# Where the projection of group C's gate stands: in group B's stage or in group A's

## The chip, the cores and the metric

One core of a Trainium2 chip runs the kernel. It has five engines with instruction queues of their own: TensorE (PE: matmuls, with its weight loads shown as PEld), VectorE (DVE), ScalarE (ACT), GpSimd (POOL) and SyncE (SP), which here issues the DMAs. Each engine works through its queue in the order in which the program wrote it. The metric is device time in microseconds (us); the median of three runs before the change is 951.26 us (949.56 to 951.63).

## The reference

Two layers of one mixer block over 512 latent tokens and 256 context tokens of width 1024. Each layer normalizes and modulates its input, projects it once to 3584 columns, and runs three kinds of attention on slices of the result: A (differential, 4 heads), B (grouped-query, 6 heads, 2 key-value heads), C (neighbourhood attention with a bias, 6 heads). Each group's output is multiplied by a gate of its own:

```python
qa, ka, va, ga, qb, kb, vb, gb, qn, kn, vn, gn = split_proj(h @ w_in[l])
...
yn = neighbourhood_attend(qn, kn, vn.reshape(b, s, C_HEADS, HEAD_DIM), kn_c, vn_c, nat_rpb[l], rows)
yn = yn * jax.nn.silu(gn)
y = jnp.concatenate([ya, yb, yn], axis=-1) @ w_out[l]
x = x + gt[:, None] * y
```

`gn` is the gate of group C: 384 columns of the projection. It needs nothing but the normalized input, and nobody needs it before C's attention is multiplied by it. In the first layer the context tokens go through everything too; in the second they only give keys and values.

## The kernel before

Tokens are cut into tiles of 128: tiles 0 to 3 are latent, 4 and 5 context. The projection is cut into chunks of columns: `a0`, `a1` (A's keys, queries, values), `ga`; `b0` (B's keys and values), `b1` (B's queries), `gb`; `c0` (C's keys), `c1` (C's values), `c2` (C's queries), `gn`. A chunk over one tile is 24 matmuls of 128x384 (8 blocks of the inner dimension, three products of split operands each: lines 684, 685, 686), a "tile" of projection below. In layer 0 `gn` has 6 tiles, in layer 1 it has 4.

After a tile's matmuls its evacuation follows. Of queries and keys: ACT copies (L467) and squares (L469), DVE sums (L470), and after every second tile one reciprocal root on POOL (L155), a scaling on DVE (L503), the split into two fp16 halves on ACT (L520, L528) and DVE (L521), and a DMA transpose issued by SP (L539). Of a gate: a tanh on ACT (L605), one DVE operation (L607) and a store to `g_d` in DRAM (L611); the attention loads it back tile by tile (L973 to L977).

A layer runs in stages. Stage A runs A's attention with the chunks of list `FA` as filler, stage B runs B's attention with `FB`, stage C runs C's attention with the output projection (`op`). The function `both` pulls filler in proportion to the attention's units: one call of `next(f)` is two inner blocks (six matmuls) of a tile. C's stage needs `c0`, `c1`, `c2` complete. In layer 0 C's attention begins with the context tiles, in layer 1 with latent rows that lie in query tiles 0 and 1.

An attention unit is: scores on TensorE (L780, `sc`) into one of two PSUM buffers, a maximum on DVE (L832, L835), the exponential on ACT (L849, which frees the scores' buffer), a split of the result into two halves (ACT L869, POOL L870 or DVE), a DMA transpose (L872, `pt<-hl`), and products with the values (L905, L906, `pv`).

Weights come through one stream: the chunks' order in `ORDER` (from the lists) is the order of 384 KB loads (L68), of the rounding on ACT (L81) and of the rest on POOL (L84), with six split pieces alive at most. Adaptive modulation (`ada`, L235 and L242; loads at L220) is a third kind of filler: while stage B of layer 0 runs, one block of it follows every second tile of projection (`st["cad"]` is 2 there and 0 in stage A), and what is left is done between stage B and stage C.

The order of the instructions on each engine is set ahead of time by a scheduler that runs its own model of the program with priorities (scores of attention come first, at -400). So a line moved in a list moves many rows.

Of the kernel before, what the change touches and what calls it, by code (L numbers as in the profile page):

```python
# [108 lines left out]
def tile_hybrid_block(ctx: ExitStack, tc: tile.TileContext, xT_d, cT_d, ng_d, w_ada, bT_d, w_in, w_out,  # L109
# [152 lines left out]
    }  # L262
    FA = ["b0", "b1", "gb"]
    FB = ["c0", "c1", "c2", "gn"]
    FC = ["y", "o"]
    YE = 2
    F1 = ["a1", "ga"]
    ORDER = [c for c in ["a0"] + F1 + FA + FB + FC if c in CH]
    VCOL = {"a0": (256, 384), "a1": (0, 128), "b0": (128, 256), "c1": (0, 384)}
# [789 lines left out]
    def both(l, g, chunks, lead=0):  # L1059
        share.phase = g  # L1060
        f = fill(l, chunks)
        nf = n_quanta(l, chunks)
        na = len(units(l, g)) + 4
        for _ in range(lead):
            next(f, None)
        done = [lead]

        def pump():
            next(f)
            done[0] += 1  # L1070

        st["pump"] = pump
        for x, _ in enumerate(attn(l, g)):
            want = min(nf, lead + (nf - lead - REST.get(g, 0)) * (x + 1) // (na - (YE if g == "B" else 0)))
            while done[0] < want:
                next(f, None)
                done[0] += 1
            if g == "B" and done[0] >= nf and st.get("y") != l:
                run(f)
                open_y(l)  # L1080
                st["y"] = l
        run(f)
# [115 lines left out]
    if True:  # L1198
# [50 lines left out]
        for l in range(DEPTH):  # L1249
# [3 lines left out]
            st["cad"] = AK[l][2]  # L1253
            both(l, "A", FA)
            st["cad"] = AK[l][3]
            both(l, "B", FB)
            while st["done"] < (24 if l == 0 else 32):
# [103 lines left out]
```

## Time and profile before

| | us |
|---|---|
| median of 3 runs | 951.26 |
| profiled execution | 952.01 |
| its span | 950.2 |
| PE busy | 834.0 |
| POOL busy | 642.8 |
| DVE busy | 652.6 |
| ACT busy | 589.5 |

The span is the time from the first to the last instruction of the profiled execution; its own time is 1.8 us longer. Busy times of an engine are sums over its instructions, with overlaps counted once. In the span layer 0 has stage A from about 108 to 264 us, stage B to about 375 and C's scores from 406; layer 1 has stage A from 624 to 739, B to 825 and C's scores from 845. The gates of C were evacuated at 388 to 425 us in layer 0 and at 840 to 866 in layer 1. In timeline rows the columns are start, length, engine, line, operation, output and inputs, and in brackets the idle time just before and who ended it. In rows of waits they are the waiting line, the one waited for, and us in total, times and longest.

### The profile page before, as it was taken

Reading aid. Unit: us, or ns where it says so; the run is one execution under the profiler, and the core shown is the slowest. Engines: PE = TensorE matmul, PEld = TensorE weight load, DVE = VectorE, ACT = ScalarE, POOL = GpSimd, SP = SyncE. Lnnn points to the kernel's source line nnn. Section 1 sums busy time; section 2 is a strip of 40 time slices with the busy share of each in tenths; the row PEclk is TensorE's granted clock in tenths of the full one; section 3 lists DMA queues with packets and bytes.
Section 4 is the critical chain, followed back from the end, with each engine's and each line's share of the span. In section 5 each row is a group of like instructions: output and inputs, shape, how many; then the busy total and the mean of one; then the engine's idle time right before and its main releaser. Section 6 shows DMA issues by size and latency. Waiting matters only on the chain.

```text
span 950.2 us, 17943 instructions
## 1 busy us (share of the span) xinstructions
PE 834.0 (88%) x6386; PEld 713.8 (75%) x6386; DVE 652.6 (69%) x1246; ACT 589.5 (62%) x1269; POOL 642.8 (68%) x562
## 2 busy tenths in 40 slices
PE   6799888979798979797999879988869999987998
PEld 4689668868676869785778669967758777875777
DVE  4977687878587577357655776567987876676543
ACT  5334587767686758476653434468868787867630
POOL 1759957997788566445444347978998995855640
PEclk8999999999899989897999978989988999998999
DMA  9925897656868977999899613467647788989732
GB/s 311 314 85 134 211 200 158 132 107 149 177 130 196 199 182 175 241 234 214 191 233 237 208 60 79 112 171 151 133 118 170 154 181 175 263 216 243 140 91 89
DMA packets 361449, 165.47 MB, mean 174 GB/s; under 512 B 256656, under 2 KB 355216, under 8 KB 361104
## 3 DMA queue, kind: packets, MB, share of 16 engines
q1 hardware_dynamic: 361360, 164.33, 73.5%
q8 instruction: 50, 0.82, 0.4%
q14 instruction: 39, 0.32, 0.1%
HBM read 86.55 MB, written 15.47 MB: 107 GB/s over the span
## 4 chain that ended last, share of the span: by engine, by line
PE 26%; POOL 10%; DMA 9%; DVE 7%; issue 4%; ACT 4%; SPq 1%; DVEq 0%; POOLq 0%; ACTq 0%
DMA pt<-hl 6%; POOL hl L870 3%; PE proj L684 3%; PE sc L780 3%; PE proj L686 3%; PE proj L685 3%; POOL wlo L84 2%; PE op L1092 2%; PE op L1094 2%; PE op L1093 2%; PE pv L905 2%; DVE mx L835 1%; ACT p L849 1%; DVE xn L503 1%; POOL rsqb L155 1%
## 5 line engine op out<-in xcount | busy, mean ns | idle before, releaser
L870 POOL TENSOR_TENSOR hl<-p,hl 128x768 f16<-128x768 f32 (+3 forms) x138 | 205.1, 1490 | 135.8 <-ACT hl L869 115.2
L84 POOL TENSOR_TENSOR wlo<-raw,whi 128x768 fp32r<-128x768 f32 (+1 forms) x104 | 184.9, 1786 | 52.6 <-ACT whi L81 31.2
L684 PE MATMUL proj<-whi,bigL 128*128 128x384 f32 (+1 forms) x592 | 203.7, 345 | 9.7 <-DVE tb L607 3.7
L685 PE MATMUL proj<-wlo,bigL 128*128 128x384 f32 (+1 forms) x592 | 199.6, 337 | 1.8 <-POOL wlo L84 1.7
L686 PE MATMUL proj<-whi,bigL 128*128 128x384 f32 (+1 forms) x592 | 196.2, 334 | 0.0
L849 ACT ACTIVATE p<-sc,nb,gsc 128x768 f32<-128x768 f32 (+3 forms) x200 | 166.9, 845 | 26.1 <-DVE p L865 14.9
L835 DVE TENSOR_REDUCE mx<-sc 128x1 f32<-128x768 f32 (+2 forms) x128 | 118.5, 930 | 32.1 <-PE sc L780 30.8
L684 PEld LDWEIGHTS proj<-whi,bigL 128*128 128x128 f32 x592 | 115.5, 195 | 19.7 <-DVE tb L607 5.7
L869 ACT CAST hl<-p 128x768 f16<-128x768 f32 (+3 forms) x144 | 104.0, 724 | 40.8 <-DMA pt<-hl 38.0
L685 PEld LDWEIGHTS proj<-wlo,bigL 128*128 128x128 f32 x592 | 115.9, 196 | 5.0 <-POOL wlo L84 2.9
L686 PEld LDWEIGHTS proj<-whi,bigL 128*128 128x128 f32 x592 | 114.8, 195 | 2.3 <-issue 1.0
L905 PEld LDWEIGHTS <-pt 128*128 128x128 f16 x736 | 68.0, 102 | 52.1 <-DMA pt<-hl 37.9
L81 ACT CAST whi<-raw 128x768 fp32r<-128x768 f32 (+1 forms) x104 | 80.7, 779 | 39.7 <-DMA raw<-in_w_in_dram 21.3
L684 PE MATMUL proj<-whi,bigC 128*128 128x384 f32 (+2 forms) x224 | 75.3, 336 | 7.0 <-ACT bigC L433 5.8
L685 PE MATMUL proj<-wlo,bigC 128*128 128x384 f32 (+2 forms) x224 | 73.6, 329 | 0.0
L905 PE MATMUL pv<-vA,pt 128*128 128x128 f16 (+2 forms) x424 | 53.8, 232 | 22.4 <-DMA pt<-hl 22.3
L155 POOL TENSOR_TENSOR rsqb<-rsqb,half 128x12 f32<-128x12 f32 (+2 forms) x25 | 70.4, 2815 | 3.2 <-DVE rsqb L154 2.9
L686 PE MATMUL proj<-whi,bigC 128*128 128x384 f32 (+2 forms) x224 | 72.5, 328 | 0.0
L906 PEld LDWEIGHTS <-pt 128*128 128x128 f16 x736 | 68.3, 102 | 3.3 <-issue 0.9
L780 PE MATMUL sc<-bigL 128*128 128x512 f16 (+4 forms) x184 | 47.6, 321 | 23.4 <-ACT p L849 20.5
L837 ACT ACTIVATE nb<-mx,lnp,gsc 128x1 f32<-128x1 f32 (+1 forms) x104 | 39.9, 385 | 35.1 <-DVE mx L835 30.5
L503 DVE TENSOR_TENSOR xn<-xn,rsqb 128x384 f32<-128x384 f32 (+1 forms) x44 | 48.6, 1130 | 15.0 <-POOL rsqb L155 10.8
(319 smaller groups left out, 2028.1 us busy)
## 6 DMA issues: line engine op xcount, KB each, us to landing
raw<-in_w_in_dram SPq DMA_DIRECT2D x56, 384.0 KB, 4.0
adw<-in_w_ada_dram SPq DMA_DIRECT2D x68, 256.0 KB, 3.7
raw<-in_w_in_dram SPq DMA_DIRECT2D x24, 256.0 KB, 3.1
raw<-in_w_out_dram SPq DMA_DIRECT2D x16, 384.0 KB, 4.7
g_d<-tb SPq DMA_DIRECT2D x20, 192.0 KB, 2.6
gt<-g_d SPq DMA_DIRECT2D x18, 192.0 KB, 2.9
hl<-in_w_ada_dram SPq DMA_DIRECT2D x12, 256.0 KB, 5.0
pt<-in_w_ada_dram SPq DMA_DIRECT2D x12, 256.0 KB, 5.0
```

What stands on the lines that cost most here:

```text
L81: self.nc.scalar.copy(out=hi, in_=raw2)
L84: self.share("W").tensor_tensor(out=lo, in0=raw2, in1=hi.bitcast(F32), op=ALU.subtract)
L155: G.tensor_tensor(out=y, in0=x, in1=half[:, 0:n], op=ALU.pow)
L684: PE.matmul(ps, lhsT=xh, rhs=hi, start=(kt == 0), stop=False)
L685: PE.matmul(ps, lhsT=xh, rhs=lo, start=False, stop=False)
L686: PE.matmul(ps, lhsT=xl, rhs=hi, start=False, stop=(kt == KT - 1))
L780: PE.matmul(ps, lhsT=q, rhs=k, start=n == 0, stop=n == b[2] - 1)
L835: V.tensor_reduce(out=mx[:, 0:ns], in_=ps[:, 0:w * ns].rearrange("p (a b) -> p a b", b=w), axis=AX.X, op=ALU.max)
L849: A.activation(out=p[:, w * x:w * x + w], in_=u["ps", i][:, w * x:w * x + w], func=AF.Exp, bias=u["nb", i][:, x:x + 1], scale=lc[l]["sc"][ ...
L869: A.copy(out=hl[:, 0:n], in_=p)
L870: lo_eng.tensor_tensor(out=hl[:, n:2 * n], in0=p, in1=hl[:, 0:n], op=ALU.subtract)
L905: PE.matmul(po[r, :], lhsT=pt[:, b, r], rhs=V_[:, vt, c0:129], start=first, stop=False)
```

## The change

The chunk `gn` goes from the end of `FB` to the end of `FA`. Nothing else changes in the text.

```diff
-    FA = ["b0", "b1", "gb"]
-    FB = ["c0", "c1", "c2", "gn"]
+    FA = ["b0", "b1", "gb", "gn"]
+    FB = ["c0", "c1", "c2"]
```

It changes what follows from the lists: stage A of layer 0 has 96 pieces of filler for its attention where it had 72, stage B has 72 where it had 96 (72 and 56, 64 and 80 in layer 1). The weights of `gn` are loaded and split ahead of those of `c0`. Stage B of layer 0 has 18 tiles of projection instead of 24, so nine modulation blocks instead of twelve come in it, and three more between B and C.

ACT, layer 0, where A's attention ends and B's begins. `sq<-proj` is the tanh of a gate tile, `xn<-proj` the copy of a tile of keys or queries, `nb<-mx,lm` belongs to A's attention and `nb<-mx,lnp` to B's. Before:

```order
L467 COPY xn<-proj 128x384
L864 ACTIVATE dn<-dn 128x1
L869 CAST hl<-p_3077 128x256
L469 ACTIVATE sq<-xn 128x384
L837 ACTIVATE nb<-mx,lm,gsc 128x2
L849 ACTIVATE p_3159,dn<-sc,nb,gsc 128x256 x2
L528 CAST stg<-xn 128x768
L862 ACTIVATE dn<-dn,lm 128x1
...
L837 ACTIVATE nb<-mx,lnp,gsc 128x1
```

After:

```order
L849 ACTIVATE p_3280,dn<-sc,nb,gsc 128x256 x2
L862 ACTIVATE dn<-dn,lm 128x1
L837 ACTIVATE nb<-mx,lm,gsc 128x2
L864 ACTIVATE dn<-dn 128x1
L849 ACTIVATE p_3327,dn<-sc,nb,gsc 128x256 x2
...
L605 ACTIVATE sq<-proj 128x384
L869 CAST hl<-p_3327 128x256
L837 ACTIVATE nb<-mx,lnp,gsc 128x1
```

The copies of `c0` that stood among the last units of A (L467, L469, L528) have given their place to the tanh of `gn` (L605); `c0` comes behind the first units of B.

PE, layer 0, ahead of the first score of C (`sc<-bigC`). Before, the last of 33 matmuls of `gn` in a row:

```order
L684 MATMUL proj<-whi,bigL 128x384
L685 MATMUL proj<-wlo,bigL 128x384
L686 MATMUL proj<-whi,bigL 128x384
L780 LDWEIGHTS bigC
L780 MATMUL sc<-bigC 128x256
```

After, behind the last matmul of `c2`, one modulation block and 20 attention products:

```order
L242 MATMUL ada<-sel,adt 128x2
L235 MATMUL ada<-adw,cS 32x128 x4
L623 MATMUL yt<-ident,o 128x128 x3
L235 MATMUL ada<-adw,cS 32x128 x4
L242 MATMUL ada<-sel,adt 128x2
L235 MATMUL ada<-adw,cS 32x128 x8
L242 MATMUL ada<-sel,adt 128x2
L235 MATMUL ada<-adw,cS 32x128
L645 MATMUL yt<-ident,xn 128x128 x4
L235 MATMUL ada<-adw,cS 32x128 x3
L780 LDWEIGHTS bigC
L780 MATMUL sc<-bigC 128x256
```

Between `c2` and C's first score stood 81 matmuls of `gn`; now modulation blocks and a few transposes of finished output rows (`yt`) stand there.

SP, layer 0, at the transposes of the last two tiles of `c2` (`bigC<-stg`). After the change:

```order
L220 DMA adw<-in_w_ada_dram 128x4x128
L68 DMA raw<-in_w_out_dram 128x3x256
L643 DMA xn<-o_d_79 128x256 x2
L220 DMA adw<-in_w_ada_dram 128x4x128
L539 DMA_TRANSPOSE bigC<-stg 128x6x128
L220 DMA adw<-in_w_ada_dram 128x4x128
L539 DMA_TRANSPOSE bigC<-stg 128x6x128
```

Before, a load of finished rows stood ahead of each of the two (L643); now a load of a modulation block does (L220), which waits until TensorE is done with the block before it.

## The prediction

> **What bounds the kernel now.** The page's shares come first.
>
> ```profile
> PE 834.0 (88%) x6386; PEld 713.8 (75%) x6386; DVE 652.6 (69%) x1246; ACT 589.5 (62%) x1269; POOL 642.8 (68%) x562
> ```
>
> TensorE is busy 88% of 950.2 us. A share over the whole span says little, so the second view is busy time by stage: layer 0 stage A (108 to 264), stage B (to 375), the passage to C (to 406.4), stage C; then layer 1 stage A, stage B, the passage, stage C and tail.
>
> ```profile
> 108.00:264.00 156.00, 133.20 (x1037) 117.99 (x1036) 120.82 (x204) 114.67 (x295) 129.17 (x126) 0.96 0.72 157
> 264.00:375.00 111.00, 99.33 (x802) 83.41 (x801) 79.50 (x144) 79.89 (x138) 77.23 (x57) 0.95 0.83 179
> 375.00:406.40 31.40, 26.43 (x220) 24.78 (x220) 14.23 (x26) 14.94 (x28) 14.44 (x9) 0.89 1.06 239
> 406.40:520.00 113.60, 103.71 (x851) 82.64 (x851) 70.26 (x164) 68.37 (x146) 55.67 (x51) 0.95 0.94 219
> 624.00:739.00 115.00, 92.46 (x663) 81.51 (x664) 93.55 (x143) 89.05 (x210) 101.17 (x99) 0.91 0.66 146
> 739.00:825.00 86.00, 80.60 (x612) 68.77 (x611) 59.70 (x81) 68.28 (x112) 70.86 (x50) 0.98 0.83 185
> 825.00:845.00 20.00, 17.52 (x142) 15.93 (x139) 15.32 (x19) 13.66 (x24) 16.42 (x9) 1.00 0.80 224
> 845.00:950.00 105.00, 94.23 (x699) 76.36 (x696) 55.49 (x127) 51.60 (x109) 41.20 (x32) 0.93 0.67 152
> ```
>
> First number after the stretch: its length, then PE busy, PEld, DVE, ACT, POOL. TensorE idles 22.8 us in stage A of layer 0 and 22.5 us in that of layer 1, where POOL (129 and 101 us) and DVE are nearly as busy, but only 11.7 and 5.4 us in stage B. So B is TensorE's, and A is shared. The third view, who TensorE waited for, tells what A's idle time is; the first two rows are layer 0's A, the next two layer 1's.
>
> ```profile
> PE pv L905 <- DMA pt<-hl: 9.3, 7, 4.3
> PE sc L780 <- ACT p L849: 4.4, 3, 2.4
> ...
> PE sc L780 <- ACT p L849: 11.8, 7, 4.2
> PE pv L905 <- DMA pt<-hl: 7.3, 4, 3.0
> ```
>
> These are waits of attention's own instructions, which stand at the head of TensorE's queue; projections behind them can't pass. More projection in the stage fills such a wait only if the written order puts it ahead of the waiting score.
>
> **The change part by part.** It removes nothing and adds nothing: 144 matmuls in layer 0 (6 tiles of 24) and 96 in layer 1, their gate evacuations (ACT tanh, DVE multiply, one store each) and four weight pieces per layer stand elsewhere. TensorE has the same work; its end moves only with its idle time. So the sum below is a ledger of idle time.
>
> *Stage A.* The order shows that gn does not go into A's holes. Before, when gb was through, TensorE went on with c0 while A's attention ran out: 83 projection matmuls stand between gb and B's first score in layer 0, 57 in layer 1. Now gn stands there: 99 and 58. The scores of A hold their places between the same tiles (A's last unit in layer 0 after 72 of these matmuls before, after 76 now). So the 22.8 and 22.5 us stay, 0 is gained, and everything from c0 on comes one gate later. Bounds: a gain of 4 where the few more matmuls meet a wait, a loss of 2 from twice as many gate tiles in a row.
>
> *What a gate weighs.* In layer 0, gn's first two tiles ran from here to the next attention product:
>
> ```profile
> 380.13 0.34 PE L686 MATMUL proj<-whi,bigC 128*128 128x384 f32 x1
> 382.74 0.42 PE L684 MATMUL proj<-whi,bigC 128*128 128x384 f32 x1
> 391.82 0.42 PE L235 MATMUL ada<-adw,cS 128*32 128x128 f32 x8 [0.36 <-DMA adw<-in_w_ada_dram]
> 406.34 1.25 PE L780 MATMUL sc<-bigC 128*128 128x256 f16 x9
> ```
>
> 380.13 is the last matmul of c2, 382.74 the first of gn; 48 of them and three products end at 391.5 (391.82 less 0.36), about 4.2 us a tile: 25 us in layer 0. The fourth row is C's first score. In these 25.9 us TensorE did 81 of gn's 144 matmuls, and attention's last products. They cover the way of c2's last tiles to C's scores, which begin with the context queries, c2's tiles 4 and 5:
>
> ```profile
> 381.64 0.48 ACT L467 COPY xn<-proj 128x384 f32<-128x384 f32 x1
> 383.81 2.91 ACT L992 ACTIVATE stB<-stB,gsc 128x768 f32<-128x768 f32 x3 [1.69 <-DMA stB<-in_btab_dram]
> 386.63 0.51 ACT L469 ACTIVATE sq<-xn 128x384 f32<-128x384 f32 x1
> 387.17 0.55 DVE L470 TENSOR_REDUCE ss<-sq 128x6 f32<-128x384 f32 x1 [4.13 <-ACT sq L469]
> 389.80 2.27 POOL L155 TENSOR_TENSOR rsqb<-rsqb,half 128x12 f32<-128x12 f32 x1
> 392.10 1.03 DVE L503 TENSOR_TENSOR xn<-xn,rsqb 128x384 f32<-128x384 f32 x2 [3.08 <-POOL rsqb L155]
> 394.51 0.50 ACT L520 CAST stg<-xn 128x384 f16<-128x384 f32 x1
> 396.16 0.54 DVE L521 TENSOR_TENSOR stg<-xn,stg 128x384 f16<-128x384 f32 x1
> 398.92 1.21 SPq L539 DMA_TRANSPOSE bigC<-stg  x1
> bigC<-stg SPq DMA_TRANSPOSE x12, 3.3
> ```
>
> From 380.4 to the landing at 398.92 + 1.21 + 3.3 = 403.4 it takes 23 us. Its own instructions, without waits, are 0.5 + 0.5 + 0.55 + 0.2 + 2.3 + 1.0 + 0.5 + 1.3 + 0.5 + 1.2 + 3.3 = 12 us. These are the bounds of the chain. In the new order the scaling of the bias table stands earlier (it cost 4.5 us here), but both transposes stand on SP's queue behind loads that wait, one after the other, for the modulation blocks on TensorE, and the second cast stands behind an evacuation of yt. I take 17 us, near the middle.
>
> *Layer 0, B to C.* c2 is now last in B. Behind it TensorE has 20 products (0.9 us by 31 in 1.4 us at 380.97), four modulation blocks (about 1.0 each, by the two rows below) and 7 transposes (about 1.3, by 0.60 for 4 at 859.50): 6.2 us.
>
> ```profile
> 380.97 0.23 PE L905 MATMUL pv<-vB,pt 128*128 128x129 f16 x1
> 380.40 0.64 PE L235 MATMUL ada<-adw,cS 128*32 128x128 f32 x16
> 382.35 0.33 PE L242 MATMUL ada<-sel,adt 128*128 128x2 f32 x2
> 859.50 0.60 PE L645 MATMUL yt<-ident,xn 128*128 128x128 f32 x4
> ```
>
> The hole is 17 - 6.2 = 10.8 us (5.8 to 16.8). The other 63 matmuls of gn (11 us) filled C's first waits; what stands there now are transposes of rows that come by DMA: 2 us more idle (0 to 6). The 5.0 us that TensorE now idles from 375 to 406.4 go. Three modulation blocks that were spread over B come together, but lie inside the hole. Together +7.8 us (+0.8 to +17.8). C's first score would come at 380.4 + 25.2 + 4.0 (88 products moved ahead) + 17 = 427, 20 us later than before, and C gets most of that back, as the 63 matmuls, 48 products and two blocks that it had to do are done.
>
> *Layer 1.* C begins with latent rows, which need c2's tiles 0 and 1 only, and tiles 2 and 3 stand between.
>
> ```profile
> 823.80 0.46 ACT L467 COPY xn<-proj 128x384 f32<-128x384 f32 x1
> 841.78 1.29 SPq L539 DMA_TRANSPOSE bigL<-stg  x1
> 844.74 0.38 PE L780 MATMUL sc<-bigL 128*128 128x256 f16 x2 [2.40 <-DVE xn L503]
> 866.67 1.11 PE L645 MATMUL yt<-ident,xn 128*128 128x128 f32 x4 [3.44 <-DVE tb L607]
> ```
>
> The chain took 21 us here. The new cover is 48 matmuls, 60 products and a turn, 8.5 + 2.6 + 0.6 = 11.7 us. With 17 the hole is 5.3 (0 to 9.3). The wait of 2.4 for the same transpose is in it and goes, and so does the 3.4 us wait of yt for gn's evacuation. A hole also costs clock:
>
> ```profile
> 703.40:706.80 3.40, 0.00 (x0) 0.00 (x0) 3.20 (x3) 1.25 (x3) 3.40 (x2) 0.84 0.28 43
> 713.60:717.00 3.40, 2.46 (x17) 2.19 (x18) 2.42 (x3) 2.86 (x8) 3.40 (x4) 0.50 0.91 70
> 720.40:724.00 3.60, 3.60 (x31) 3.18 (x31) 3.44 (x6) 1.12 (x3) 2.19 (x3) 1.00 0.64 164
> 395.00:398.00 3.00, 0.59 (x2) 0.50 (x2) 1.83 (x5) 0.01 (x1) 0.16 (x1) 0.52 1.12 288
> ```
>
> After an idle stretch the granted clock was 0.50 and came back to 1.00 once TensorE had been busy. Work of 1.7 us loses as much again; I take 1 us for layer 1. In layer 0 the passage has such a stretch already (0.52 at 395). The Trainium skill, "TensorE: Matmul & The Clock Gate", Part 1, says that the clock is halved after an idle window of about 3.4 us and released after a busy one, which speaks against any change that opens a hole; the rows agree. By that rule both holes would pay 1.7 us, an estimate of 1.7 + 0.7 = 2.4 us over my sum. Layer 1: 5.3 - 2.4 - 3.4 + 1 = +0.5 us (-5.8 to +5.2).
>
> *Stage B's own waits* shrink a little, since products stand further behind their scores: -1 us (-3 to 0).
>
> Sum: 0 + 7.8 + 0.5 - 1 = **+7.3 us**. The profiled execution took 952.01 us for its span of 950.2, 0.75 over the median of 951.26, so the difference is added to the median: **958.5 us**. All low ends together give -12, all high ends +25.
>
> **Rivals.** *The chain is covered (faster).* ACT and DVE have little else at the end of B now, so the chain could run at 12 us, and C's early waits need not grow. Then layer 0 is 5.8 + 0 - 5.0 = +0.8, layer 1 0 - 5.8, B -3: -8, 943 us. For it: DVE was busy 14.2 of 31.4 us there. Against: SP's queue and a DMA share of 1.06.
>
> *A takes gn into its idle time*, as the words of the change say. If half of the 45.3 us in both layers were filled, the time would be 929 us. Against it is the order of the scores. A part of it sits in the faster case's chance.
>
> *TensorE isn't the bound (no change).* If C's pace is attention's, and the passage's hole is work that waited elsewhere anyway, the changes cancel within 0.2% (1.9 us, about what a measurement of this kernel can tell): 951 us. The Trainium skill, "Perfetto Trace Analysis", Identifying the Most-Contended Engine, says that matmul busy share misleads and weight-load share is the measure. That share is 75% here, 83.4 of 111 us in stage B. By it TensorE would have room, and this case a better chance. Against: in layer 1's passage there is no gap but the one of 2.4 us.
>
> *C doesn't get its time back (much slower).* C starts 20 us later in layer 0 and some 15 in layer 1 (12.4 of work moved ahead, less 2.4, plus 5.3); if its units go at attention's own pace, half of the 16 us of moved work in layer 0 and a third of the 12 in layer 1 are not recovered: 7.3 + 8 + 4 = +19, 970 us. It decides once C's scores wait for ACT rather than TensorE; from 420 to 520 that wait is this one row, which speaks against it.
>
> ```profile
> PE sc L780 <- ACT p L849: 2.2, 1, 2.2
> ```
>
> **How the numbers follow.** Forecast (+2 to +15) 0.52; much slower 0.12; no change 0.15; faster 0.21. So slower 0.64, same 0.15, faster 0.21, and the likeliest is 958.5, in its own range 953.5 to 966. To leave out 2 in 10 the range runs from 945 (the covered chain less some) to 971 (the much slower case).
>
> **What would show it.** In the changed profile: a TensorE gap of 6 to 17 us ahead of C's first score in layer 0, with c2's last transposes landing just before; that score at about 427; gate evacuations at about 245 to 285 and not at 388 to 425; idle time of A unchanged within 4 us in both layers; a gap under 9 us ahead of layer 1's first C score; C from first score to end shorter by 10 to 16 us. I am wrong if A's idle time falls by 10 us or more, if the gap in layer 0 is under 5 us, or if C takes as long as before.

## The result and the profile after

The changed kernel took 959.48 us (median of 12 runs) where the kernel before took 951.44 us beside it: a ratio of 1.0074, 95% interval 1.0045 to 1.0103. One of the twelve runs, 973.87 us at a mean granted clock of 0.81 where the others read 0.93 to 0.95, was in a slower state of the chip and is left out of the ratio, which is one of means. By the ratio the change is slower by 7.0 us, by the medians by 8.0; 958.5 us was forecast. The amount is right. Its place is not, as the following shows.

The profiled execution of the change took 957.69 us, its span 955.9. The shares on its page hardly differ:

```profile
PE 836.5 (88%) x6386; PEld 714.3 (75%) x6386; DVE 638.0 (67%) x1246; ACT 588.9 (62%) x1269; POOL 634.5 (66%) x562
```

The view of busy time by stage tells more. The stretches are cut at first and last scores: layer 0's stage A, B, the passage from B's last score to C's first, C to the end of the layer; then layer 1 to C's first score, and C. Columns as before (length, PE, PEld, DVE, ACT, POOL, clock, DMA share, GB/s). The change:

```profile
108.70:264.10 155.40, 133.42 (x1032) 116.95 (x1032) 123.08 (x204) 111.68 (x289) 120.14 (x122) 0.99 0.67 156
264.10:373.20 109.10, 103.23 (x863) 88.95 (x863) 70.63 (x139) 81.22 (x138) 82.06 (x61) 1.00 0.90 188
373.20:423.20 50.00, 33.69 (x305) 28.27 (x304) 22.66 (x52) 21.20 (x42) 18.91 (x11) 0.83 0.98 233
423.20:624.10 200.90, 181.75 (x1322) 153.13 (x1320) 128.21 (x285) 104.46 (x234) 112.12 (x101) 0.92 0.66 165
624.10:857.90 233.80, 203.92 (x1514) 180.35 (x1515) 164.08 (x250) 175.28 (x354) 190.80 (x159) 0.93 0.73 173
857.90:955.90 98.00, 86.30 (x593) 67.16 (x593) 54.61 (x117) 47.80 (x99) 35.55 (x28) 0.85 0.53 127
```

The same cuts of the kernel before, from C of layer 0 on (the first three differ by under 1 us from rows shown with the prediction):

```profile
406.30:624.20 217.90, 198.09 (x1465) 167.80 (x1463) 138.42 (x306) 111.23 (x246) 119.45 (x105) 0.93 0.71 175
624.20:844.70 220.50, 190.32 (x1407) 165.94 (x1407) 168.21 (x241) 170.99 (x344) 188.25 (x156) 0.95 0.74 168
844.70:950.20 105.50, 94.49 (x699) 76.62 (x699) 55.79 (x128) 51.60 (x109) 41.20 (x32) 0.93 0.67 151
```

Layer 1 begins at 624.1 us with the change and at 624.2 before. So in these two executions layer 0 lost nothing, though its C began 17 us later, and all of the difference in span, 5.7 us, came up in layer 1: 331.8 us against 326.0.

The hole ahead of layer 0's first C score is there, and larger than forecast. TensorE's timeline in the changed kernel, with c2's last matmul and the score at the ends:

```profile
400.58 0.34 PE L686 MATMUL proj<-whi,bigC 128*128 128x384 f32 x1
410.81 0.65 PE L235 MATMUL ada<-adw,cS 128*32 128x128 f32 x8 [8.15 <-DMA adw<-in_w_ada_dram]
414.69 0.66 PE L235 MATMUL ada<-adw,cS 128*32 128x128 f32 x8 [0.45 <-DMA adw<-in_w_ada_dram]
416.36 0.66 PE L235 MATMUL ada<-adw,cS 128*32 128x128 f32 x8 [1.02 <-DMA adw<-in_w_ada_dram]
421.02 0.61 PE L235 MATMUL ada<-adw,cS 128*32 128x128 f32 x2 [3.00 <-DMA adw<-in_w_ada_dram]
423.18 0.61 PE L780 MATMUL sc<-bigC 128*128 128x256 f16 x2
```

12.6 us of idle time in brackets, all for loads of the left-over modulation blocks, of 16.3 us that TensorE idles in the whole passage. SP's own timeline in the same stretch shows c2's two transposes standing among these loads:

```profile
405.65 0.93 SPq L220 DMA_DIRECT2D adw<-in_w_ada_dram  x2
...
417.18 0.38 SPq L220 DMA_DIRECT2D adw<-in_w_ada_dram  x1
417.61 1.76 SPq L539 DMA_TRANSPOSE bigC<-stg  x1
419.46 0.53 SPq L220 DMA_DIRECT2D adw<-in_w_ada_dram  x1
420.03 1.25 SPq L539 DMA_TRANSPOSE bigC<-stg  x1
```

The second transpose is issued at 421.3 and lands some 2 us later, so the last block and the last transpose are done together.

The first left-over block also held c2's own chain. The root for c2's last two tiles ended on GpSimd at 407.5 us, but their scaling (L503) began on VectorE at 413.5. Ahead of it in VectorE's queue stood the evacuation (L628) of three transposes (L623), and on TensorE these stand behind the block that waited 8.15 us for its load:

```profile
405.22 2.27 POOL L155 TENSOR_TENSOR rsqb<-rsqb,half 128x12 f32<-128x12 f32 x1 [0.35 <-DVE rsqb L154]
411.40 0.90 PE L623 MATMUL yt<-ident,o 128*128 128x128 f32 x3
412.33 0.48 ACT L627 CAST bigC<-yt 128x384 fp32r<-128x384 f32 x1 [8.36 <-PE yt L623]
412.85 0.56 DVE L628 TENSOR_TENSOR bigC<-yt,bigC 128x384 fp32r<-128x384 f32 x1 [6.92 <-ACT bigC L627]
413.52 2.04 DVE L503 TENSOR_TENSOR xn<-xn,rsqb 128x384 f32<-128x384 f32 x2
```

In layer 1 the waits ahead of C's first scores are smaller:

```profile
853.89 0.88 PE L623 MATMUL yt<-ident,o 128*128 128x128 f32 x3 [2.51 <-DVE o L950]
857.89 0.58 PE L780 MATMUL sc<-bigL 128*128 128x256 f16 x2 [3.12 <-DMA bigL<-stg]
```

### The profile page after: what moved, and what is told of

It is laid out like the page before. It is cut to its first block, busy times and chain, and to the rows that moved or that the text cites. A ratio compares the mean times of both kernels' runs of the same rounds, so it can differ in the third digit from the quotient of the medians.

```text
span 955.9 us, 17984 instructions
## 1 busy us (share of the span) xinstructions
PE 836.5 (88%) x6386; PEld 714.3 (75%) x6386; DVE 638.0 (67%) x1246; ACT 588.9 (62%) x1269; POOL 634.5 (66%) x562
## 4 chain that ended last, share of the span: by engine, by line
PE 25%; DVE 9%; DMA 8%; POOL 6%; issue 6%; ACT 5%; SPq 1%; DVEq 0%; POOLq 0%; ACTq 0%
PE proj L684 3%; PE sc L780 3%; PE proj L685 3%; PE proj L686 3%; POOL hl L870 2%; PE op L1092 2%; ACT p L849 2%; PE op L1093 2%; PE op L1094 2%; DMA pt<-hl 2%; DMA raw<-in_w_in_dram 2%; DMA adw<-in_w_ada_dram 2%; DVE xn L503 1%; POOL wlo L84 1%; PE pv L905 1%
## 5 line engine op out<-in xcount | busy, mean ns | idle before, releaser
L870 POOL TENSOR_TENSOR hl<-p,hl 128x768 f16<-128x768 f32 (+3 forms) x138 | 202.3, 1470 | 130.8 <-ACT hl L869 122.6
L686 PEld LDWEIGHTS proj<-whi,bigL 128*128 128x128 f32 x592 | 114.5, 194 | 2.4 <-issue 1.1
L905 PEld LDWEIGHTS <-pt 128*128 128x128 f16 x736 | 65.9, 99 | 36.6 <-DMA pt<-hl 18.9
L906 PEld LDWEIGHTS <-pt 128*128 128x128 f16 x736 | 66.6, 100 | 4.2 <-issue 1.4
L780 PEld LDWEIGHTS <-bigL 128*128 128x128 f16 (+2 forms) x344 | 24.7, 103 | 42.5 <-issue 30.7
```

The lines of the kernel that those rows point to most:

```text
L686: PE.matmul(ps, lhsT=xl, rhs=hi, start=False, stop=(kt == KT - 1))
L780: PE.matmul(ps, lhsT=q, rhs=k, start=n == 0, stop=n == b[2] - 1)
L870: lo_eng.tensor_tensor(out=hl[:, n:2 * n], in0=p, in1=hl[:, 0:n], op=ALU.subtract)
L905: PE.matmul(po[r, :], lhsT=pt[:, b, r], rhs=V_[:, vt, c0:129], start=first, stop=False)
```

## The experiments

Times are medians; ratios are of means, to the kernel before that ran beside them, with 95% intervals. So a ratio isn't the quotient of two medians of the table.

| kernel | time, us | ratio | layer 0, us | layer 1, us |
|---|---|---|---|---|
| before | 951.44 | 1 | 516.0 | 326.0 |
| the change | 959.48 | 1.0074 (1.0045 to 1.0103) | 515.4 | 331.8 |
| gn in A in layer 0 alone | 951.23 | 0.9978 (0.9958 to 0.9998) | 521.9 | 323.0 |
| gn in A in layer 1 alone | 956.77 | 1.0041 (1.0022 to 1.0060) | 515.7 | 329.7 |
| change, three blocks in A | 950.81 | 0.9972 (0.9949 to 0.9996) | 511.9 | 329.4 |
| change, c2 early, three blocks in A | 943.30 | 0.9891 (0.9858 to 0.9924) | 497.2 | 330.4 |
| layer 1 alone, c2 early there | 959.40 | 1.0068 (1.0039 to 1.0097) | 516.5 | 330.0 |
| before, three blocks left over | 954.26 | 1.0016 (0.9993 to 1.0039) | 512.1 | 328.7 |
| before, c2 early | 937.70 | 0.9830 (0.9797 to 0.9863) | 504.7 | 325.4 |
| change, c2 early | 953.76 | 1.0003 (0.9977 to 1.0029) | 506.7 | 329.9 |
| the change again | 953.33 (one) | | 515.2 | 328.4 |
| before, c2 early, gn in C in layer 1 | 936.65 | 0.9838 (0.9815 to 0.9861) | 501.3 | 326.3 |
| before, c2 early, three blocks in A | 934.97 | 0.9816 (0.9791 to 0.9841) | 501.9 | 325.0 |
| gn in A in layer 0 alone, c2 early, three blocks in A | 936.68 | 0.9851 (0.9813 to 0.9890) | 499.2 | 326.9 |

"Layer 0" is, in each profiled execution, from layer 0's first score of A to layer 1's, and "layer 1" from there to the end. One execution each: three of the same layer 0 (before, and the two edits of layer 1 alone) read 515.7 to 516.5, three of the changed one 515.2, 515.4 and 521.9. The execution profiled need not be typical: that of "change, c2 early" took 946.52 us, the shortest of its twelve. Since the scheduler plans everything anew, an edit in one layer also reorders rows of the other. The layer 0 of the edit in layer 1 alone has TensorE's rows in the order of before, and that of the edit in layer 0 alone has them in the order of the change. Their layers 1 have the lists of the change and of before, but many rows stand in another order there.

**Layer 0 alone, layer 1 alone.** The lists were made per layer (the diff shows the lists alone, and the comment gives the second kernel; the order of the weights and the calls of the stages follow them):

```diff
-    FA = ["b0", "b1", "gb"]
-    FB = ["c0", "c1", "c2", "gn"]
+    IN_A = {0: 1, 1: 0}      # and {0: 0, 1: 1}
+    FAL = {l: ["b0", "b1", "gb"] + ["gn"] * IN_A[l] for l in range(DEPTH)}
+    FBL = {l: ["c0", "c1", "c2"] + ["gn"] * (1 - IN_A[l]) for l in range(DEPTH)}
```

> gn moves to stage A in layer 0 alone; layer 1 as before the change. The prediction's sum put +7.8 us into layer 0's passage from B to C and +0.5 into layer 1. Theory (the lost cover in layer 0's passage): the loss of about 8 us stays whole, 957 to 961 us, with the same TensorE waits for modulation loads of 10 us or more ahead of C's first score. Rival (the loss comes from layer 1, where the changed profile shows waits of 2.5 and 3.1 us ahead of C's first scores): 951 to 954 us.

> gn moves to stage A in layer 1 alone. Theory (layer 0 holds the loss): within 3 us of before, 949 to 954 us. Rival (layer 1): 955 us or more.

The theory fell in both. With gn moved in layer 0 alone the time was 0.22% under before, with the hole in place: C's first score at 423.7 us, as in the change. With gn moved in layer 1 alone it was 0.41% over. Stage B and the passage of the kernel changed in layer 0 alone:

```profile
265.10:374.70 109.60, 103.53 (x864) 89.03 (x863) 72.55 (x139) 81.11 (x139) 81.71 (x61) 1.00 0.90 188
374.70:423.70 49.00, 33.82 (x305) 28.26 (x303) 22.70 (x52) 21.32 (x42) 19.28 (x11) 0.83 0.99 234
```

Stage B has 6.1 us of idle TensorE time where it had 11.7, and the clock is 1.00 where it was 0.95. The profile of the change reads 5.9 and 1.00.

The two edits don't add up to the change: -0.22% and +0.41% make +0.19%, about 2 us, where the change has 7. In the profile of the edit in layer 0 alone layer 0 is even 5.9 us longer than before, and it is layer 1, with the lists of before in another order, that is 3.0 us shorter. So these two runs don't show that the move costs nothing in layer 0; they show that the time of a kernel with the hole need not be over that of before.

**The left-over modulation blocks.** Three blocks of layer 0 are done in stage A, one after every eighth tile, on top of the change; and, the other way round, the kernel before leaves three over to be done behind stage B:

```diff
-AK = [[6, 2, 0, 2], [0, 1, 0, 2]]
+AK = [[6, 2, 8, 2], [0, 1, 0, 2]]
```

```diff
-                if st["cad"] and st["n"] % st["cad"] == 0:
+                if st["cad"] and st["n"] % st["cad"] == 0 and not (l == 0 and share.phase == "B" and st["done"] >= 21):
```

> The change, with three modulation blocks of layer 0 done in stage A (one after every eighth tile), so that none is left over between B and C. In the changed profile TensorE waited 12.6 us for modulation loads ahead of C's first score. Theory 1 (c2 is last and its chain to the transposes is bare, the loads only fill the same time): a hole stays, 8 us or more of idle time or of waits for c2's transposes, C's first score 15 us or more behind c2's last matmul, 955 to 960 us. Theory 2 (the three blocks left over make the hole, as each load waits for the block before, and c2's transposes stand behind these loads on SP's queue): TensorE idles under 5 us there, C's first score comes within 14 us, 949 to 954 us.

> Before the change, but with three modulation blocks of layer 0 left over for the passage from B to C, as the change leaves them; gn stays at the end of stage B. Theory 1 (the blocks' loads cost where nothing covers them): here gn covers them, 949 to 955 us. Theory 2 (the left-over blocks cost by themselves, by late modulation or by SP's queue): 956 us or more.

With the blocks in stage A the change is 0.28% under before, and 1.0% under itself. Its waits from 366 us to C's first score, and that score:

```profile
PE yt L623 <- DMA xn<-o_d: 4.4, 4, 2.0
PE yt L645 <- DMA xn<-o_d: 4.2, 3, 1.9
PE pv L905 <- DMA pt<-hl: 1.3, 2, 0.8
```

```profile
399.80 0.34 PE L686 MATMUL proj<-whi,bigC 128*128 128x384 f32 x1
418.34 0.84 PE L780 MATMUL sc<-bigC 128*128 128x256 f16 x3
```

Both theories were half right. The score still comes 18.2 us behind c2's last matmul, as theory 1 had it: c2's chain is bare. But TensorE works meanwhile, since the transposes of finished rows (`yt`) moved up to where the blocks had stood; it waits 8.6 us for their loads, in small pieces, and idles 11.4 us in the passage for 16.3. The scaling of c2's last tiles now begins 1.0 us behind its root, where the change has 6.0:

```profile
404.31 2.33 POOL L155 TENSOR_TENSOR rsqb<-rsqb,half 128x12 f32<-128x12 f32 x1 [0.35 <-DVE hb L565]
407.61 1.02 DVE L503 TENSOR_TENSOR xn<-xn,rsqb 128x384 f32<-128x384 f32 x2
```

The time is theory 2's. Before the change, leaving three blocks over costs nothing that can be told (0.16%, interval from -0.07% to 0.39%), and C's first score came even a little earlier. But gn does not cover them there. In the profile they stand behind that score, in C's first waits:

```profile
403.68 1.58 PE L780 MATMUL sc<-bigC 128*128 128x256 f16 x12 [1.90 <-DMA bigC<-stg]
L235 PE MATMUL ada<-adw,cS x48: 272/297/421, 421.8 to 436.7; 128*32 128x128 f32 x48
```

The second row is of all blocks from 418 to 437 us: three blocks of 16 matmuls, with the first and last start. So three blocks cost 1.0% ahead of C's first score, behind c2, and, in the order of before, nothing that can be told behind that score. That they would cost nothing under gn's cover is argued, not shown.

**c2 ahead of c1.** C's values are needed by no score, so they can cover the way of its queries. In the change with the blocks in stage A, in the change alone, and in the kernel before (whose list ends with "gn", as the comment says):

```diff
-    FB = ["c0", "c1", "c2"]            # before: [..., "gn"]
+    FB = ["c0", "c2", "c1"]            # before: [..., "gn"]
```

> The change, with c2 ahead of c1 in stage B, so that the values of C (which no score needs) cover c2's way to the scores, and the three modulation blocks done in stage A. Theory (cover of the passage is what was lost, stage A costs nothing): no gap over 3 us ahead of C's first score in either layer, that score within 25 us of B's last one, 946 to 952 us. Rival (gn in stage A delays B and C for a reason of its own, such as gate evacuations in a row or the weights' order): still 956 us or more.

> The change with c2 ahead of c1, and nothing done about the left-over blocks. Theory (the late c2 alone makes the loss): 941 to 948 us, as with the blocks moved. Rival (the left-over blocks are a loss of their own here, some 3 to 8 us, as 0.7 to 1% lay between the change with and without them): 948 to 953 us.

> Before the change, with c2 ahead of c1; gn stays at the end of stage B. The version with c2 ahead of c1, gn in stage A and three blocks in stage A took 1.09% less than before. Theory (what counts is how early c2 is; where gn stands then matters little): 941 to 948 us. Rival (gn out of stage B is a gain of its own, once c2 is covered): 949 to 953 us.

All three start C early: its first score follows B's last one by 14.3, 9.4 and 5.1 us in layer 0, where it was 50 in the change and 31 before. In the last of them TensorE is full in between:

```profile
372.00:377.10 5.10, 5.10 (x45) 4.64 (x43) 1.48 (x2) 5.01 (x11) 3.73 (x3) 1.00 1.18 260
```

The kernel before with c2 early is 1.70% faster than before, the best that one edit gave: the place of c2 was worth far more than that of gn. On the change the same edit gives 0.7%, and 1.8% with the blocks moved too. The times missed their forecasts: 943.30 and 937.70 us came out lower than either theory, and 953.76 higher than the theory and just above the rival. Without the blocks moved, these fall into C's start. TensorE's longest waits there, without and with the blocks moved:

```profile
PE ada L235 <- DMA adw<-in_w_ada_dram: 3.8, 3, 2.1
```

```profile
PE sc L780 <- DMA bigC<-stg: 3.1, 1, 3.1
PE ada L242 <- DVE adt L240: 2.1, 1, 2.1
```

The 3.1 us are the wait ahead of C's first score itself. So the waits at C's start don't explain the 9.5 us by which layer 0 is longer with the blocks there. By the stages TensorE idles 5.7 us more in stage A, 4.5 more in B, 5.7 more in C and 4.1 less in the passage; why, stays open.

**c2 early in layer 1 alone.** In the kernel changed in layer 1 alone:

```diff
+    FBL = {l: (["c0", "c2", "c1"] if l else ["c0", "c1", "c2"]) + ["gn"] * (1 - IN_A[l]) for l in range(DEPTH)}
```

> Layer 0 word for word as before; in layer 1 gn in stage A and c2 ahead of c1 in stage B. With gn in stage A of layer 1 alone the time was 0.41% over before, with C's first score 16.6 us later than before, after a TensorE wait of 5.0 us. Theory (in layer 1 the loss is the late first score of C, since c2 is last): the score comes earlier than before the change (under 840 us), no wait over 2 us ahead of it, and the time falls to before or below, 946 to 953 us. Rival (gn in stage A costs in stage A or B of layer 1, by gate evacuations or the weights' order): still 955 us or more.

The diff shows the one list that differs. The theory fell: C's first score came at 840.3 instead of 861.3, 1.9 us behind B's last one, and the time stayed 0.68% over before. Layer 1 to C's first score and from it, with c2 late and then early:

```profile
622.90:861.30 238.40, 203.93 (x1511) 180.36 (x1512) 169.72 (x249) 175.12 (x353) 189.83 (x160) 0.93 0.74 170
861.30:952.60 91.30, 82.07 (x596) 63.75 (x596) 50.56 (x118) 47.98 (x100) 35.27 (x28) 0.91 0.55 136
```

```profile
624.70:840.30 215.60, 184.59 (x1338) 162.33 (x1338) 161.33 (x237) 163.97 (x337) 179.59 (x153) 0.91 0.72 158
840.30:954.70 114.40, 101.55 (x770) 82.78 (x769) 56.66 (x131) 58.48 (x116) 44.67 (x34) 0.94 0.70 165
```

21 us earlier, and 23 us longer from there. In layer 1 the late first score is not the loss. In both profiles stage A of layer 1 took 119.8 us, where it took 115.2 before, as the rival had it; but in the two profiles of the change itself it took 114.5 and 114.1, so this isn't the loss of the change either.

**The change once more, and three combinations.**

> The changed kernel once more, for a second profile. In the profiles so far, from layer 1's first score of A to the end took 329.4 to 331.8 us in all six orders with gn in stage A there, and 323.0 to 328.7 us in four with gn in stage B; layer 0 from first to first score took 515.4 and 521.9 us in the changed order, 515.7 to 516.5 us in the old one (three profiles). Theory (layer 1 holds the larger part of the loss): layer 1 between 329 and 333 us again, layer 0 between 513 and 523. Rival (the split is chance, the prediction's layer 0 has it): layer 1 under 328 us, layer 0 over 522.

The second profile of the change has 515.2 us for layer 0 and 328.4 for layer 1, a little below the band named for layer 1 and above that of the rival. Its stage B, passage and last stage:

```profile
262.80:372.60 109.80, 103.22 (x865) 89.00 (x864) 70.67 (x139) 81.82 (x139) 81.98 (x61) 1.00 0.89 189
372.60:421.50 48.90, 33.68 (x304) 28.18 (x301) 22.68 (x52) 20.65 (x42) 18.93 (x11) 0.83 0.98 233
...
855.40:951.60 96.20, 83.15 (x593) 64.74 (x593) 54.63 (x117) 47.88 (x99) 35.61 (x28) 0.91 0.55 129
```

Idle times of 6.6 and 15.2 us and both clocks of layer 0 repeat. The last stage doesn't: its clock was 0.85 in the first profile and 0.91 in this one, and it is 1.8 us shorter.

The combinations, all with c2 early: gn at the head of stage C's filler in layer 1; gn in stage B with three blocks in stage A; gn in stage A in layer 0 alone with three blocks there. Of the first one the diff shows the call of stage C, with gn taken off the list of stage B in layer 1:

```diff
-            both(l, "C", FC + ["n"] * (l + 1 == DEPTH))
+            both(l, "C", ["gn"] * l + FC + ["n"] * (l + 1 == DEPTH))
```

> c2 ahead of c1 and layer 0 as in the version with gn in stage B (1.70% under before); in layer 1 gn goes one stage later, to the head of stage C's filler. Theory (in layer 1 late filler is worth more than early filler, as C's attention waits and A's cannot be filled): layer 1 from first score to end 318 to 326 us, time no more than with gn in stage B, 932 to 938 us. Rival (there is a best place and it is stage B's end; in C gn delays the output projection, which sets the end): 940 us or more.

> c2 ahead of c1, gn at the end of stage B, and three modulation blocks of layer 0 in stage A. With gn in stage A in both layers and c2 early, moving the blocks took 1.1% off. Theory (the blocks' loads are costly wherever they stand in B and its end): 928 to 935 us. Rival (only blocks left over for the passage cost, and with gn in B none are): 935 to 940 us, as without.

> c2 ahead of c1 in both layers, gn in stage A in layer 0 alone, three blocks of layer 0 in stage A. Layer 0 took 497.2 us from first to first score in this order, layer 1 took 325.4 us with gn in stage B and c2 early. Theory (the layers add up): 108 + 497 + 325 = 930 us of span, 927 to 936 us. Rival (layer 0's gain came from one execution): 938 us or more.

They took 1.62%, 1.84% and 1.49% less than before, which can't be told from each other or from the 1.70% of c2 early alone. The second time, 934.97, lies on the border of its two forecasts and the third, 936.68, between its two, so neither decides. gn in stage C is as good as in stage B in layer 1, so later is not better without end; with gn in stage B the blocks may stay where they are; and gn in stage A of layer 0 is no gain, where the layers' sum of single executions (930 us) had let one hope. The fastest median is 934.97 us, with c2 ahead of c1, gn in stage B and three blocks in stage A.

## Why the prediction was right in amount and wrong in place

*Stage A* stood as forecast: idle time of 22.0 us (23.0 in the second profile) in layer 0 where it was 22.8, and 19.7 (19.8) in layer 1 where it was 22.3. gn did not go into the holes, it took c0's place. "A takes gn into its idle time" is refuted.

*Layer 0, B to C, +7.8 us.* The hole was there, at 423 us for a forecast 427. The idle time of the passage went from 5.0 to 16.3 us (15.2 in the second profile): +11, above the +5.8 that the term had for the passage (10.8 less 5.0; its other 2 us were for C's first waits) and inside its bounds. The chain took 22.3 us for 17 taken, near the upper end of 23. I had the left-over blocks "inside the hole"; they lengthened it. With them in stage A the chain took 18.2 us, close to the 17, and ahead of C the first block's load delayed the scaling of c2 by some 5 us, by way of the transposes behind it. Moving them away took 1.0% off the whole.

*Stage B, -1 us*, is the step that failed for layer 0. Its idle time fell from 11.7 to 5.9 us (6.6 in the second profile, 6.1 with layer 0 changed alone), beyond my bound of -3, and the clock rose from 0.95 to 1.00 in all three. c2's last matmul ended at 400.9 us, not at the 409.6 of the working: 8.7 us were given back ahead of the hole. I had summed idle time at constant work, and left the clock of a fuller stage out of layer 0's sum, though I had put a clock term into layer 1's. With +11 in the passage and -5 to -6 of idle time and about 5 of clock in B (0.05 of 111.9 us, an estimate), layer 0 comes out near zero: 515.4 and 515.2 us against 515.7 to 516.5. The idle half of this repeats, the clock's half does not: in three executions of the changed layer 0 TensorE idled 63.3, 64.4 and 63.4 us for 59.3 before, while its work took 452.1, 450.8 and 458.4 us for 456.8. The third of these, at 521.9 us, did not get its hole back.

*Layer 1, +0.5 us*, is the other step that failed. With gn in stage A layer 1 took 328.4 to 331.8 us in seven profiles, mean 329.9; with gn in stage B 323.0 to 328.7 in six, mean 325.8. That is +4.1 us, whatever the place of c2, within the bounds of my term and far from its middle. Its hole was of the forecast size: 2.5 and 3.1 us of waits where 5.3 was taken, and TensorE's idle time between B's last and C's first score went from 2.4 to 5.6 us. But removing that hole (c2 early) removed nothing of the loss, so the term's mechanism isn't its cause. In the first profile of the change the idle time of layer 1 is that of before within 1 us, and its work took 5.4 us longer at a clock of 0.85 in the last stage; in the second profile the work is as before and the idle time 2.4 us more. On average the loss is not in stage A, where gn now stands: from layer 1's first score to B's first one the seven profiles took 116.7 us and the six 117.3, and from there to the end 213.3 and 208.5. But no stage shows it in all profiles, and what carries it stays open.

*C gets most of it back* held in layer 0, where C to the layer's end was 17 us shorter, and less in layer 1, 7.5 of 13 us. "Much slower" is refuted, and "no change" came true in layer 0 alone, in the two profiles of the change. "The chain is covered" is refuted for the change, but it names what the version with c2 early does on purpose.

So two terms were off by about -8 and +4 us. That leaves some 3 us of the forecast 7.3, and the two profiles of the change are 5.7 and 1.4 us over that of before, so the division by layer does not account for the 7.0 measured. The agreement between 7.3 and 7.0 is luck.

## What to carry to other kernels

Ask of a filler what it stands in front of before moving it away: here the last filler covered two chains of transfers, and moving the chain's start forward (c2 ahead of c1, 1.7%) was worth more than any place of the filler. A rule that doles out side work by a count of other work leaves a remainder when that count changes; look where the remainder lands and what waits behind it in the same queue, here by way of a third engine: TensorE waited for a load, transposes waited behind it, and VectorE held c2's scaling behind their evacuation. A hole in one stage is not its price: sum the stages on both sides, with the clock, and check the end of the layer, not the end of the hole.

## What the runs showed of the hardware

In one stage the granted clock of TensorE went with how densely it was filled, and by the estimate above that was about as large as the idle time itself: stage B of layer 0 read 1.00 in three profiles of the denser order (5.9 to 6.6 us idle) and 0.95 before (11.7 us); the passage read 0.83 with the hole and 0.89 before. It does not go with the idle time everywhere: stage A of layer 0 read 0.96 before with 22.8 us idle, and 0.99 and 1.00 in the change with 22.0 and 23.0. The same program in the same order had 0.85 in its last stage once and 0.91 the second time. A single profile's division of a loss by stage is therefore good to a few us only: the same layer 0 took 515.2, 515.4 and 521.9 us.
